# Making the low parts of the weights with an accumulating DMA instead of a subtraction

## The chip, the cores and the metric

The kernel runs on one core of one Trainium2 chip. The metric is the device time of one execution in microseconds, shown as the median of repeated runs. A profile of one execution goes with it: what each engine did and when, what each wait ended on, and what the DMA queues moved.

The engines are named as the profile names them. PE is the matrix engine, with PEld for its weight loads; DVE the vector engine; ACT the scalar engine; POOL the general engine, which can also issue DMAs; SP the engine that here issues all DMAs of the kernel before. Each takes its own instructions strictly in the order in which they were laid down: one that waits holds up all behind it on that engine, while the others go on.

## The reference, cut to what matters

One layer of a decoder over 512 prompt tokens and 32 sample tokens (eight batches of four), all in float32: half a feed-forward block, a mixing layer (half of its heads a recurrent RWKV-7 group, half differential attention), and half a feed-forward block again, with a norm before and after each.

```python
def swiglu(x, w_in, w_out):
    gate, up = jnp.split(x @ w_in, 2, axis=-1)
    return (jax.nn.silu(gate) * up) @ w_out

def layer(x, l, shift0, wkv0, attend, P):
    g = P['norm_gains'][l]
    h = x + 0.5 * rms_norm(swiglu(rms_norm(x, g[0], NORM_EPS), P['ff1_in'][l], P['ff1_out'][l]), g[1], NORM_EPS)
    m, k, v, wkv, shift = mixer(rms_norm(h, g[2], NORM_EPS), l, shift0, wkv0, attend, P)
    h = h + rms_norm(m, g[3], NORM_EPS)
    h = h + 0.5 * rms_norm(swiglu(rms_norm(h, g[4], NORM_EPS), P['ff2_in'][l], P['ff2_out'][l]), g[5], NORM_EPS)
    return h, k, v, wkv, shift
```

Six weight matrices carry the work: `ff1_in`, `ff2_in` (1024 x 5632), `ff1_out`, `ff2_out` (2816 x 1024), `w_in` (1024 x 3328, the projections ahead of the mixer) and `w_out` (1024 x 1024, behind it).

## The kernel before, in words

The 544 tokens are two halves of 272; activations lie with features on the partitions. A weight tile is one block of 128 output features for all its input features, 128 x 1024 float32 (512 KB), or 128 x 768 for the last group of the second feed-forward matrix.

**Two parts for each number.** The matrix engine takes float32r, a shorter form. So every weight and every activation is split in a high part (the value rounded to float32r) and a low part (the value less its high part, rounded too), and a product is the sum of three: high x high, high x low, low x high. `dot` computes one tile's product for one half of the tokens in 24 matmuls: for each of eight 128-row pieces high x high (L130) and high x low (L131), and behind these 16 the eight with the weights' low part (L134). `mm3` (L121 to L123) does the same three piece by piece. So the low part of a weight is wanted only for the last third of a `dot`.

**Making the parts.** `weights` loads a tile into `wraw` (three buffers) by a DMA on SP, lets ACT copy it to `whi` (L114, which rounds), and lets POOL subtract `whi` from `wraw` into `wlo` (L116). `whi` and `wlo` have four buffers each (`wx`, a pool of four more, takes the second half of the tiles in the last group of each feed-forward block). A buffer comes free when the last matmul that reads it is done. For `w_out` the subtraction alternates between DVE and POOL. The first two tiles of the kernel are not made by `weights`, but by hand (L413 to L425).

**The stages.** A feed-forward block (`ff`) goes through 22 blocks of hidden features in three groups. For each hidden block it takes two weight tiles (gate and up), four `dot`s; DVE scales the results (L386, L387), ACT applies Silu (L357), DVE multiplies (L358), ACT and DVE split the hidden rows (L141, L143). After each group, `products` multiplies by the second matrix: eight tiles, two `dot`s each. Between the blocks come the 26 tiles of `w_in` (`proj`, two `dot`s each), mixed with the preparation of the recurrence on DVE (among it the 31 dependent steps of a triangular inverse, L691 and L693), then the recurrence and the attention, which have no weights, and at last `output`: the eight tiles of `w_out` for half 0, and, loaded anew, for half 1, one `dot` for each tile. Its results leave PSUM by ACT (L1224). While half 1 goes through, `close_half` finishes half 0: norm (L276), residual (L277, on POOL for some blocks and on DVE for the others), and the split of the next block's input (L246, L248). `opening` is the first products of a block, with four weight tiles.

**What sets the order.** A scheduler lays down each engine's order from its own estimate of when things are ready; the waits follow from who writes and reads each buffer. So another cost or wait in `weights` also moves instructions elsewhere.

Of the kernel before, what the change touches and what calls it, by code (L numbers as in the profile page):

```python
# [51 lines left out]
def build(ctx, tc, A):  # L52
# [38 lines left out]
    # matmuls ahead of the first data, so that the tensor engine's clock is up when it comes  # L91
# [15 lines left out]
    # ---------------------------------------------------------------- helpers  # L107
    def weights(src, n, wx=None, eng=G, raw=None):
        if raw is None:
            raw = wp.tile([128, n], FT, name="wraw", bufs=3, padded_shape=[128, 1024])  # L110
            nc.sync.dma_start(raw, src)
        slot = dict(bufs=4, padded_shape=[128, n if wx else 1024])
        hi = (wx or wp).tile([128, n], FR, name="whi", **slot)
        S.activation(hi, raw, AF.Copy)  # L114
        lo = (wx or wp).tile([128, n], FR, name="wlo", **slot)
        eng.tensor_tensor(lo, raw, hi.bitcast(FT), op=OP.subtract)  # L116
        return hi, lo

    def mm3(ps, w, x, first, last):
        """ps (+)= w.T @ x, each the exact sum of two float32r parts"""  # L120
# [4 lines left out]
    def dot(ps, w, xs, k0=0, ins=None):  # L125
        """ps = the sum over k of w[k].T @ xs[k], the parts of the weights that come last at the end"""
# [37 lines left out]
    def sums(pt, src, cols):  # L164
        """sums over the partitions that each of cols marks, of a half's tokens, which go on the partitions"""
# [4 lines left out]
    def sums4(ps, bank):  # L170
        """a half's sums, 32 rows (two times 16 alike) for each of four tiles, turned round: [token, tile, block, sum]"""
# [7 lines left out]
    def inv_sqrt(pt, n, scale=1.0, eps=None, least=None, y=None):  # L179
        """(scale * pt + eps) ** -0.5, or of at least `least`: a guess from the exponent, a step of  # L180
        the third order (two thirds of its result), a Newton step"""
# [23 lines left out]
    def spread(y, e, bank=bank):  # L205
        """tokens back to the free axis: each of a token's e values on its share of the partitions, in PSUM"""
# [30 lines left out]
    class Pre:  # L237
        """a block's input, gains applied; the rows' scale is left to whoever takes the product out"""
# [23 lines left out]
    def close_half(h, s, y, sq, gcol, pre=None, xp=None, spill=None, out=None):  # L262
        """the sub-layer's norm and residual, then the next one's input; in steps that other work goes between"""
# [44 lines left out]
    def opening(ws, xs, take):  # L308
        """the first products with a new input: half 1's side by side, as its rows get ready; taken out unscaled"""
# [14 lines left out]
    def products(wsrc, x, y, finish, per=1, wx=None, apart=False):  # L324
        """y[m] for all m and both halves, of weights that hold `per` m each; apart: half 1 after all of half 0"""
# [81 lines left out]
    # ---------------------------------------------------------------- first half-step  # L407
# [46 lines left out]
    # ---------------------------------------------------------------- token mixing  # L454
# [11 lines left out]
    # what lives from the projections to the output product  # L466
# [25 lines left out]
    def projected(i):  # L492
        """block i of the projected RWKV columns, behind the token before: what proj takes, what shifted reads"""
# [28 lines left out]
    def shifted(pr, dst, dsts):  # L522
        """mixed with the token before"""
# [55 lines left out]
    # negated biases over distances  # L579
# [10 lines left out]
    # a row for each partition, so that reading one place earlier on each gives a Toeplitz matrix  # L590
# [5 lines left out]
    for b in range(4):  # L596
# [14 lines left out]
        # decays: products over the chunk, of all tokens up to one and including it  # L611
# [6 lines left out]
        # removal keys, of unit length  # L618
# [11 lines left out]
        # keys and their share  # L630
# [45 lines left out]
    # unit triangular inverses: 32x32 blocks on one partition each, then one merge  # L676
# [25 lines left out]
    def merged():  # L702
        """the inverses' lower left blocks, in steps between the projections"""
# [27 lines left out]
    # queries, and in their place what they attend to  # L731
# [3 lines left out]
    # ---------------------------------------------------------------- RWKV, prompt: chunk after chunk  # L735
# [5 lines left out]
    def ahead(c, bank):  # L741
        """what a chunk needs from its own tokens alone"""
# [22 lines left out]
        # right-hand sides: keys against values  # L765
# [9 lines left out]
    def chunk(c, state, ar, g, kbt, vs, rhs):  # L775
        # the state's part of the right-hand sides
# [14 lines left out]
        # next state  # L791
# [7 lines left out]
        # outputs  # L799
# [11 lines left out]
    # ---------------------------------------------------------------- attention projections  # L811
# [13 lines left out]
    def between(spot):  # L825
        """a step of the inverses' merging behind the products so far"""
        if spot in ((1, 0), (1, 1), (1, 2), (2, 0)):
            with tc.issue_after(latest[0]):
                next(merging, None)
# [41 lines left out]
    # ---------------------------------------------------------------- attention, prompt  # L871
    # lambda
# [11 lines left out]
    # negated biases: one Toeplitz tile for each head  # L884
# [5 lines left out]
    # a head's two queries, each with zeros for the other's rows  # L890
# [40 lines left out]
    # ---------------------------------------------------------------- RWKV, samples: one small chunk  # L931
    sm = att.enter_context(tc.tile_pool(name="smp", bufs=1, side="right", reuse_waits="tile"))

    def sample_steps():
# [14 lines left out]
        # state against keys and queries, value-major: [v, (which, batch, t)]  # L949
# [90 lines left out]
    # ---------------------------------------------------------------- attention, samples  # L1040
    sa = att.enter_context(tc.tile_pool(name="sat", bufs=1, side="right", reuse_waits="tile"))

    def past_steps():
# [12 lines left out]
        # biases of the rows (batch, head, map, t): buckets of all t stacked on the partitions  # L1056
# [23 lines left out]
        def pages(src, n, j0, i):  # L1080
            """two pages of one batch, in a slot of the weights"""
# [315 lines left out]
```

## Time and profile before

| | |
|---|---|
| median of three runs | 1316.78 us (1316.12 to 1322.76) |
| profiled execution, first to last instruction | 1314.4 us |
| PE busy | 1256.5 us, 96% |
| DVE busy | 696.4 us, 53% |
| POOL busy | 503.1 us, 38%; 399.9 of it in L116 |
| ACT busy | 461.2 us, 35%; 182.6 of it in L114 |
| DMA | 142.06 MB, queue q1 34.4% of 16 engines' span |

A row of instruction groups reads: line, engine, operation, output<-inputs, shapes, count | busy us, mean ns of one | idle time of the engine just before, and what ended it. A row of waits reads: who waited, for whom: us in total, times, longest. Time that an engine spends waiting counts only where PE, which has by far the most work, stands still for it.

### The profile page before, as it was taken

The page shows a single profiled execution, that of the slowest core. Times are in us where ns is not written, and L with a number is a line of the kernel's source. Part 1 is how long each engine was busy: PE and PEld are TensorE (multiplying, and loading weights), DVE is VectorE, ACT ScalarE, POOL GpSimd, SP SyncE. Part 2 cuts the span into 40 slices and gives each one's busy share as a digit, 9 for nine tenths or more (in the row PEclk, how much of TensorE's full clock was granted, in tenths as well). Part 3 has the DMA queues.
Part 4 walks back from the last instruction along what each step waited for, and adds up shares of the span by engine and source line. Part 5 has one row for each costly group of instructions (what it writes and reads, how often), then busy time and mean ns, then how long its engine had stood idle before and what let it go on. Part 6 is the DMA issues. An engine that isn't in the chain of part 4 may idle for free.

```text
span 1314.4 us, 25021 instructions
## 1 busy us (share of the span) xinstructions
PE 1256.5 (96%) x10354; PEld 1184.2 (90%) x10354; DVE 696.4 (53%) x1356; ACT 461.2 (35%) x878; POOL 503.1 (38%) x330
## 2 busy tenths in 40 slices
PE   8999999999998989989999999998899999999996
PEld 7999999999998888978887755888899999999995
DVE  7742034412448898879425367788842044412446
ACT  6433232312334444411114446555332233312331
POOL 2534433443346496633000022343534343433342
PEclk8999999999999999899899899999999999999998
DMA  5333223322232423353116357541323322322221
GB/s 198 99 95 97 81 81 97 95 83 81 85 109 87 150 87 124 135 180 110 59 50 190 129 177 262 182 131 47 113 81 97 94 79 86 97 85 79 82 61 68
DMA packets 54455, 142.06 MB, mean 108 GB/s; under 512 B 6050, under 2 KB 17058, under 8 KB 53191
## 3 DMA queue, kind: packets, MB, share of 16 engines
q1 hardware_dynamic: 54342, 140.48, 34.4%
q8 instruction: 81, 1.33, 0.4%
q14 instruction: 32, 0.25, 0.1%
HBM read 125.05 MB, written 16.72 MB: 108 GB/s over the span
## 4 chain that ended last, share of the span: by engine, by line
PE 45%; DVE 9%; ACT 1%; DMA 1%; issue 1%; SPq 0%; DVEq 0%; POOL 0%; ACTq 0%
PE mm L134 7%; PE mm L131 7%; PE mm L130 7%; PE pb L134 3%; PE pb L131 3%; PE pb L130 3%; DVE sqa L228 1%; PE pb L905 1%; DVE tmp L691 1%; PE pb L807 1%; PE pb L806 1%; PE pb L755 1%; DVE X L693 1%; PE pb L927 1%; PE mm L1099 1%
## 5 line engine op out<-in xcount | busy, mean ns | idle before, releaser
L116 POOL TENSOR_TENSOR wlo<-wraw,whi 128x1024 fp32r<-128x1024 f32 (+1 forms) x168 | 399.9, 2384 | 540.7 <-ACT whi L114 488.3
L130 PE MATMUL mm<-xh,whi 128*128 128x272 f32 x1160 | 303.1, 292 | 9.1 <-DVE q_f L820 3.5
L131 PE MATMUL mm<-xl,whi 128*128 128x272 f32 x1160 | 303.5, 293 | 4.7 <-DVE xl L248 4.7
L114 ACT ACTIVATE whi<-wraw 128x1024 fp32r<-128x1024 f32 (+1 forms) x176 | 182.6, 1039 | 253.8 <-PE mm L131 152.0
L130 PEld LDWEIGHTS mm<-xh,whi 128*128 128x128 f32 x1160 | 221.6, 191 | 11.3 <-DVE q_f L820 4.1
L131 PEld LDWEIGHTS mm<-xl,whi 128*128 128x128 f32 x1160 | 221.7, 191 | 6.6 <-DVE xl L248 6.3
L134 PE MATMUL mm<-xh,wlo 128*128 128x272 f32 x1160 | 179.4, 298 | 0.0
L134 PEld LDWEIGHTS mm<-xh,wlo 128*128 128x128 f32 x1160 | 162.8, 197 | 0.3
L130 PE MATMUL pb<-xh,whi 128*128 128x272 f32 x568 | 150.5, 295 | 1.6 <-ACT ga L371 0.9
L131 PE MATMUL pb<-xl,whi 128*128 128x272 f32 x568 | 149.2, 294 | 0.0
L358 DVE TENSOR_TENSOR up<-up,ga 128x272 f32<-128x272 f32 x88 | 111.7, 1271 | 8.2
L130 PEld LDWEIGHTS pb<-xh,whi 128*128 128x128 f32 x568 | 110.3, 194 | 2.8 <-ACT ga L371 1.1
L131 PEld LDWEIGHTS pb<-xl,whi 128*128 128x128 f32 x568 | 109.9, 194 | 0.3 <-issue 0.2
L387 DVE TENSOR_TENSOR up<-mm,rpre 128x272 f32<-128x272 f32 x54 | 23.8, 442 | 114.9 <-PE mm L134 114.8
L134 PE MATMUL pb<-xh,wlo 128*128 128x272 f32 x568 | 83.2, 288 | 0.0
L134 PEld LDWEIGHTS pb<-xh,wlo 128*128 128x128 f32 x568 | 75.6, 188 | 0.0
L357 ACT ACTIVATE ga<-ga 128x272 f32<-128x272 f32 x88 | 38.0, 432 | 71.5 <-DVE ga L386 63.4
L386 DVE TENSOR_TENSOR ga<-mm,rpre 128x272 f32<-128x272 f32 x53 | 23.2, 438 | 73.7 <-PE mm L134 73.7
L130 PE MATMUL mm<-hd0h,whi 128*128 128x272 f32 x242 | 62.0, 289 | 0.0
L131 PE MATMUL mm<-hd0l,whi 128*128 128x272 f32 x242 | 61.9, 288 | 0.0
L130 PE MATMUL mm<-hd1h,whi 128*128 128x272 f32 x220 | 56.4, 289 | 0.0
L131 PE MATMUL mm<-hd1l,whi 128*128 128x272 f32 x220 | 56.3, 288 | 0.0
(406 smaller groups left out, 2277.5 us busy)
## 6 DMA issues: line engine op xcount, KB each, us to landing
wraw<-in_ff_in_dram SPq DMA_DIRECT2D x87, 512.0 KB, 3.6
wraw<-in_ff_out_dram SPq DMA_DIRECT2D x32, 512.0 KB, 3.6
wraw<-in_w_in_dram SPq DMA_DIRECT2D x26, 512.0 KB, 3.9
pg<-in_cache_k_dram SPq DMA_DIRECT2D x32, 256.0 KB, 3.7
pg<-in_cache_v_dram SPq DMA_DIRECT2D x32, 256.0 KB, 5.1
wraw<-in_w_out_dram SPq DMA_DIRECT2D x16, 512.0 KB, 4.1
wraw<-in_ff_out_dram SPq DMA_DIRECT2D x16, 384.0 KB, 3.2
cat_d<-cat SPq DMA_DIRECT2D x4, 1280.0 KB, 5.0
```

The lines of the kernel that those rows point to most:

```text
L114: S.activation(hi, raw, AF.Copy)
L116: eng.tensor_tensor(lo, raw, hi.bitcast(FT), op=OP.subtract)
L130: T.matmul(ps, hi, xs[k][0], start=k == 0, stop=False)
L131: T.matmul(ps, hi, xs[k][1], start=False, stop=False)
L134: latest[0] = T.matmul(ps, wcols(w, k0 + k)[1], xs[k][0], start=False, stop=k == n - 1).ins
L228: eng.tensor_tensor(self.acc, self.acc, sq, op=OP.add)
L357: S.activation(g, g, AF.Silu)
L358: V.tensor_tensor(u, u, g, op=OP.mult)
L386: V.tensor_tensor(g, pg, pre.rs[s], op=OP.mult)
L387: V.tensor_tensor(u, pu, pre.rs[s], op=OP.mult)
L691: V.tensor_tensor(tv, lb[:, j + 1:, j:j + 1].to_broadcast([128, n, m]), X[:, j:j + 1, :m].to_broadcast([128, n, m]), op=OP.mult)
L693: V.tensor_tensor(X[:, j + 1:, :m], X[:, j + 1:, :m], tv, op=OP.subtract)
```

## The change

The low part is no longer computed by an engine. ACT writes the raw weights a second time, times -1 and rounded, into `wlo`: that is minus the high part. Then a DMA issued from POOL reads the raw tile again from DRAM and adds it onto `wlo` in place. Both are the same value as before: raw less high. The options for another engine and for a raw tile that is there already go with it, so `w_out` is treated like the rest. The two tiles made by hand at the start stay as they were. (The new file also drops comments and docstrings; in it the load is L110, the two passes of ACT are L113 and L115, and the DMA is L116.)

```diff
-    def weights(src, n, wx=None, eng=G, raw=None):
-        if raw is None:
-            raw = wp.tile([128, n], FT, name="wraw", bufs=3, padded_shape=[128, 1024])
-            nc.sync.dma_start(raw, src)
+    def weights(src, n, wx=None):
+        raw = wp.tile([128, n], FT, name="wraw", bufs=3, padded_shape=[128, 1024])
+        nc.sync.dma_start(raw, src)
         slot = dict(bufs=4, padded_shape=[128, n if wx else 1024])
         hi = (wx or wp).tile([128, n], FR, name="whi", **slot)
         S.activation(hi, raw, AF.Copy)
         lo = (wx or wp).tile([128, n], FR, name="wlo", **slot)
-        eng.tensor_tensor(lo, raw, hi.bitcast(FT), op=OP.subtract)
+        S.activation(lo, raw, AF.Copy, scale=-1.0)
+        G.dma_start(lo, src, accum_op=OP.add)
         return hi, lo
...
-            w = weights(A["w_out"][m], 1024, eng=(V, G)[m % 2])
+            w = weights(A["w_out"][m], 1024)
```

The order on ACT in the middle of the first feed-forward block, before and with the change (`ga` and `up` are the two hidden tiles, `hd0h` and `hd1h` the high parts of the hidden rows of the two halves):

```order
L357 ACTIVATE ga<-ga 128x272
L141 ACTIVATE hd0h<-up 128x272
L114 ACTIVATE whi<-wraw 128x1024
L357 ACTIVATE ga<-ga 128x272
L114 ACTIVATE whi<-wraw 128x1024
L141 ACTIVATE hd1h<-up 128x272
```

```order
L357 ACTIVATE ga<-ga 128x272
L141 ACTIVATE hd0h<-up 128x272
L113 ACTIVATE whi<-wraw 128x1024
L115 ACTIVATE wlo<-wraw 128x1024
L357 ACTIVATE ga<-ga 128x272
L113 ACTIVATE whi<-wraw 128x1024
L115 ACTIVATE wlo<-wraw 128x1024
L141 ACTIVATE hd1h<-up 128x272
```

Each tile's second pass stands right behind its first; the Silu and the split of the hidden rows stand behind both.

ACT again, in `output` for half 0 (`my` are its results, `sq` their squares), before and with the change:

```order
L1224 ACTIVATE my_1_9641<-pb 128x272
L227 ACTIVATE sq<-my_1_9641 128x272
L114 ACTIVATE whi<-wraw 128x1024
L1224 ACTIVATE my_2_9642<-mm 128x272
L227 ACTIVATE sq<-my_2_9642 128x272
```

```order
L113 ACTIVATE whi<-wraw 128x1024
L1224 ACTIVATE my_1_9733<-mm 128x272
L115 ACTIVATE wlo<-wraw 128x1024
L227 ACTIVATE sq<-my_1_9733 128x272
L113 ACTIVATE whi<-wraw 128x1024
```

Here the second pass stands behind the copy of a product out of PSUM.

POOL from the first tiles of `w_out` to the first of `ff2_in` (`yr` is the recurrence's output, `h` the residual), before and with the change:

```order
L116 TENSOR_TENSOR wlo<-wraw,whi 128x1024
L1192 TENSOR_TENSOR yr<-yr,gor 128x272 x2
L116 TENSOR_TENSOR wlo<-wraw,whi 128x1024 x3
L277 TENSOR_TENSOR h_9928<-h_9928,pn 128x272
L116 TENSOR_TENSOR wlo<-wraw,whi 128x1024
L277 TENSOR_TENSOR h_9928<-h_9928,pn 128x272 x2
L116 TENSOR_TENSOR wlo<-wraw,whi 128x1024
L277 TENSOR_TENSOR h_9928<-h_9928,pn 128x272
```

```order
L1192 TENSOR_TENSOR yr<-yr,gor 128x272 x6
L116 DMA wlo<-in_w_out_dram 128x1024 x12
L277 TENSOR_TENSOR h_10028<-h_10028,pn 128x272 x3
L116 DMA wlo<-in_ff_in_dram 128x1024
L277 TENSOR_TENSOR h_10028<-h_10028,pn 128x272
L116 DMA wlo<-in_ff_in_dram 128x1024 x3
```

The residual of half 0 (L277), which had stood between the subtractions, stands behind the last DMA for `w_out`.

## The prediction

> **What bounds the kernel now.** The page first: busy shares. Then the table by stretches, cut where the stages change (per row: PE's busy time and matmuls, then PEld, DVE, ACT, POOL, the granted clock, the DMA engines' share, GB/s).
>
> ```profile
> PE 1256.5 (96%) x10354; PEld 1184.2 (90%) x10354; DVE 696.4 (53%) x1356; ACT 461.2 (35%) x878; POOL 503.1 (38%) x330
> ...
> 40.00:400.00 360.00, 359.37 (x2869) 359.16 (x2867) 135.23 (x200) 111.21 (x177) 150.63 (x65) 1.00 0.32 91
> 400.00:640.00 240.00, 214.66 (x1810) 203.89 (x1811) 202.20 (x391) 84.66 (x146) 129.58 (x141) 0.93 0.38 124
> 640.00:800.00 160.00, 160.00 (x1679) 116.97 (x1679) 72.54 (x231) 61.93 (x183) 11.59 (x16) 0.97 0.45 141
> 800.00:960.00 160.00, 146.91 (x1065) 130.87 (x1064) 127.15 (x252) 82.83 (x170) 66.12 (x37) 0.98 0.41 130
> 960.00:1280.00 320.00, 320.00 (x2555) 320.00 (x2555) 107.34 (x168) 94.40 (x147) 129.04 (x56) 1.00 0.29 85
> ```
>
> In the two feed-forward blocks PE never stops, so nothing that POOL or DVE saves there can be seen. One matmul comes every 320/2555 = 0.125 us: a `dot` of 24 is 3.0 us, a tile with two `dot`s 6.0 us. PE stands still for 25.3 us between 400 and 640 (projections, recurrence's preparation) and for 13.1 us between 800 and 960 (output product, opening of the second block); there DVE is busy for 84% and 79%. The waits of PE in these two stretches, longest first:
>
> ```profile
> PE pb L214 <- DVE rx L209: 5.7, 3, 2.0
> PE pb L214 <- DVE ry L202: 4.0, 2, 2.2
> PE mm L130 <- DVE q_f L820: 3.5, 3, 1.7
> PE mm L131 <- DVE xl L248: 3.4, 2, 2.4
> PE pb L709 <- DVE lb L697: 2.8, 1, 2.8
> ...
> PE pb L255 <- DVE sqa L228: 2.6, 1, 2.6
> PE pb L168 <- DVE sqa L228: 2.3, 1, 2.3
> PE mm L130 <- DVE ga L386: 1.9, 1, 1.9
> ```
>
> These rows are 26.2 us, all on DVE. No row of PE waits for POOL, and none for the low part of a weight. So the subtractions of POOL, though 400 us long, are hidden; what they cost, they cost through DVE:
>
> ```profile
> L116 POOL TENSOR_TENSOR wlo<-wraw,whi 128x1024 fp32r<-128x1024 f32 (+1 forms) x168 | 399.9, 2384 | 540.7 <-ACT whi L114 488.3
> L358 DVE TENSOR_TENSOR up<-up,ga 128x272 f32<-128x272 f32 x88 | 111.7, 1271 | 8.2
> ...
> 28.60 0.44 DVE L358 TENSOR_TENSOR up<-up,ga 128x272 f32<-128x272 f32 x1
> ...
> 589.83 2.39 DVE L693 TENSOR_TENSOR X<-X,tmp 128x135 f32<-128x135 f32 x1
> 592.25 0.32 DVE L691 TENSOR_TENSOR tmp<-lb,X 128x156 f32<-128x156 f32 x1
> ...
> 589.67 2.40 POOL L116 TENSOR_TENSOR wlo<-wraw,whi 128x1024 fp32r<-128x1024 f32 x1 [3.77 <-PE mm L134]
> ```
>
> The multiplication L358 takes 0.44 us at 28.60, where POOL is idle, and 1.27 us in the mean. At 589.83 a step of the inverse that is smaller than its neighbour takes 2.39 us instead of 0.3: it started 0.16 us after a subtraction on POOL and ended with it. A DVE operation with two inputs in SBUF that meets a subtraction waits until that is over.
>
> **The subtractions go.** 168 on POOL and 8 on DVE (in `output`). On POOL this is off the path: worth nothing by itself. Through DVE, bounds: nothing, if PE's waits have other causes, and all 26.2 us of the rows above. The longest waits are 1.7 to 2.8 us each, about one blocked operation (2.1 us in the pair at 589.83); 26 and 21 subtractions fall in the two stretches, and without them DVE still has 202 - 26 x 2.1 = 147 us of work in the 240 of the first. I take two thirds: **-18 us**.
>
> **ACT's second pass.** 176 more passes of 1.04 us:
>
> ```profile
> L114 ACT ACTIVATE whi<-wraw 128x1024 fp32r<-128x1024 f32 (+1 forms) x176 | 182.6, 1039 | 253.8 <-PE mm L131 152.0
> ...
> 942.94 1.01 PE mm L134 x8
> ```
>
> 183 us on an engine that is busy for 461 of 1314. In 960 to 1280 it is 2555/48 = 53 tiles, 55 us on top of 94 in 320: hidden under PE; without that cover it would be 1 us per tile. The added wait: L115 needs the buffer of `wlo`, free after the last L134, while L113 needs that of `whi`, free after the last L131. The eight L134 take 1.01 us, L113 itself 1.04, so L115 finds it free. Behind both in the feed-forward blocks stand the Silu and the split of the hidden rows, then DVE's L143, then the products, which come a group later: nothing. In `output` the copies out of PSUM (L1224) stand between the passes, and three PSUM buffers of 3 us each cover a delay of 1 us. **0**, up to +2 where PE has just lost its lead.
>
> **The DMA's load.** A second read of 176 tiles, now with an addition. No row shows such a DMA. The plain one:
>
> ```profile
> q1 hardware_dynamic: 54342, 140.48, 34.4%
> ...
> wraw<-in_ff_in_dram SPq DMA_DIRECT2D x87, 512.0 KB, 3.6
> ...
> wraw<-in_w_out_dram SPq DMA_DIRECT2D x16, 512.0 KB, 4.1
> ...
> h_d<-h SPq DMA_DIRECT2D x2, 1088.0 KB, 10.8
> h<-h_d SPq DMA_DIRECT2D x2, 1088.0 KB, 5.2
> ```
>
> Of the 16 engines, 0.344 x 1314.4 us went for 140.48 MB, so 1.69 us for 0.524 MB. The addition reads the tile from DRAM, reads `wlo` and writes it: at least one pass (1.69), at most three one after the other (5.07). I take two, 3.4 us, since a plain load's read and write are one pass already and one read comes on top. Then a tile takes 1.69 + 3.4 = 5.1 of PE's 6.0 us: hidden, at 85% of the DMA engines. At three it is 6.8 and the DMA engines become the bound (below).
>
> The Trainium skill has a price (Collectives: The Full Stack, "The bandwidth ceiling"): an adding DMA is slower not for the addition but for its two source reads on one ring, 62.28 against 32.35 GB/s, 1.93 times. By it, as an estimate, the tile would take 1.69 + 3.26 = 4.95 us, and the sum stays. No run here shows it yet.
>
> **The DMA's delay.** The low part was there 2.39 us after the high one; now it takes L115, an issue on POOL and a landing. Bounds for the landing: 3.6 us (a plain load) and 10.8 us (the slowest row, twice the bytes). I take 7, twice the plain load. What it may take follows from four buffers. In a feed-forward block a buffer of the first tile of a pair is free after the third of four `dot`s (9.0 us), and its next low part is wanted 16 matmuls into the next pair but one (24 + 2.0): 17 us, less 1 for L115. In `output`, with one `dot` for each tile, it is free after 3.0 and wanted at 12 + 2.0: 11 us, less L115 and the copy ahead of it (0.4): 9.5. So 7 us is hidden in both; at 10.8 `output` loses 1.3 us in each round of four, 5 us in all.
>
> The cover is thin where a block opens, since all four tiles are wanted at once. At the start of the program:
>
> ```profile
> 17.18 1.05 ACT L114 ACTIVATE whi<-wraw 128x1024 fp32r<-128x1024 f32 x1
> ...
> 23.16 1.17 PE L134 MATMUL pb<-xh,wlo 128*128 128x272 f32 x8
> ```
>
> Ready now at 17.18 + 2.1 + 7 = 26.3, wanted at 23.16: 3 us late, which products of the other half can fill in part. Three such openings: **+3** (0 to 9). In `output` the DMA engines, at 0.41 of 160 us before, get 21 tiles' additions of 3.4 us on top (0.86), and loads that DVE waits for (the recurrence's rows) share them; POOL's residual of half 0 now comes behind twelve DMAs, each waiting for ACT. **+5** (0 to 20).
>
> ```profile
> SPq L111 <- POOL wlo L116: 789.8, 149, 26.1
> ```
>
> SP's loads wait for POOL to be done with `wraw`; now ACT releases it 1.3 us earlier. The loads are a buffer ahead anyway: nothing.
>
> **Sum**: -18 + 0 + 3 + 5 = -10 us on a profiled span of 1314.4, so 1304.4. The median of the runs is 2.4 us above that span; against it the forecast is 1307 us.
>
> **Rivals.** *The saving stays on DVE.* PE's waits end on DVE, but the chain in front of them is long, and what DVE wins is lost at the openings and behind the second pass: 1316. For it: in 400 to 640 transfers stand in the chain of waits too:
>
> ```profile
> 572.68 7.28 DMA bon_d<-bon
> 580.46 3.86 DMA ar<-cat_d
> ```
>
> Against it: the inverse, a pure DVE chain, with single steps of 2.1 us too much.
>
> *The low parts come late.* One mechanism, in `output` and the three openings: landing over 9.5 us, because the additions queue with the loads at 85% load. At 14 us, four rounds of 4.5 us in `output` and 7 us more at each opening are 18 + 21 = 39, against -10: about 1345. For it: the store of 10.8 us, and DMA shares of 0.38 to 0.45 ahead of the change in the middle stages. Against it: loads that land in 3.6 us at today's load.
>
> *The addition takes three passes.* From 4.3 us per tile on (6.0 - 1.69) the feed-forward blocks hang on the DMA engines; at 5.07 each of their 136 tiles takes 0.78 us longer: +106, with -10 about 1412. For it: no row shows an addition. Against it: nothing but the count of reads.
>
> *The change does not free DVE*, since POOL's writing of descriptors blocks it too: the -18 goes, 1324. By the Trainium skill (SBUF — State Buffer, "Who interferes with whom") a DVE operation with two SBUF inputs meets only a GpSimd instruction that reads SBUF, not one that only writes: this rival would then be out. The trace shows the reading half (589.83, 2.39 us) alone.
>
> **How the numbers follow.** Forecast 0.47, saving stays on DVE 0.18, low parts late 0.20, three passes 0.10, DVE not freed 0.05. The likeliest has its own range of 1290 to 1311: from all 26.2 us with no loss, to 6 us left of them. The range to hold 8 of 10 goes down to 1290 and up to 1365, past the late low parts and short of three passes. About 0.5% (6.6 us) is what a measurement of this kernel tells from no change. Faster by more: 0.45, the forecast without its upper rim. Slower by more: 0.20 + 0.10 and a part of the two cases near zero, 0.34. Within: 0.21.
>
> **What would show it.** Right: L358's mean falls from 1.27 to under 0.6 us; in 400 to 640 and 800 to 960 PE's busy time rises by 12 us or more together, and its waits on DVE shrink; the feed-forward stretches stay at 0.125 us per matmul; POOL's busy time is near 100 us, ACT's near 644. The step on load: the DMA share in 960 to 1280 near 0.29 x 3 = 0.87; over 0.95 with PE waiting is three passes. The step on delay: additions that land in 7 us; a PE wait named for L134 and `wlo` means late low parts. The forecast falls if PE's waits on DVE stay as they are, or new ones on DMAs come to more than they lose.

## The result, and the profile after

The changed kernel takes 1338.61 us (median of four runs, 1333.09 to 1340.21) against 1318.97 us before: a ratio of 1.0139, 95% interval 1.011 to 1.0169. It is 1.4% slower; the forecast was 0.7% faster. The profiled execution spans 1338.5 us.

From the page of the changed kernel, and for L358 from its groups of DVE: the busy shares, groups of instructions, DMA queues (packets, MB, share of 16 engines' span) and DMA issues (count, KB each, median us from issue to landing).

```profile
PE 1275.5 (95%) x10354; PEld 1194.5 (89%) x10354; DVE 527.3 (39%) x1348; ACT 618.0 (46%) x1054; POOL 249.9 (19%) x338
...
L115 ACT ACTIVATE wlo<-wraw 128x1024 fp32r<-128x1024 f32 (+1 forms) x176 | 181.5, 1033 | 5.8 <-PE mm L134 5.0
L116 POOL DMA_DIRECT2D wlo<-in_ff_in_dram x86 | 74.6, 871 | 416.9 <-ACT wlo L115 402.6
...
L358 DVE TENSOR_TENSOR up<-up,ga 128x272 f32<-128x272 f32 x88 | 38.8, 442 | 8.5 <-ACT ga L357 0.5
...
q0 software_dynamic: 25344, 90.19, 36.4%
...
wraw<-in_ff_in_dram SPq DMA_DIRECT2D x87, 512.0 KB, 5.2
wlo<-in_ff_in_dram POOLq DMA_DIRECT2D x86, 512.0 KB, 7.9
...
wlo<-in_w_in_dram POOLq DMA_DIRECT2D x26, 512.0 KB, 8.9
...
wraw<-in_w_out_dram SPq DMA_DIRECT2D x16, 512.0 KB, 8.6
```

DVE is freed as forecast: L358 takes 442 ns, not 1271, and DVE is busy 169 us less. ACT's second passes are 181.5 us; as neighbouring rows overlap a little, ACT is busy 156.8 us more. The additions cost 0.364 x 1338.5 us of the 16 engines for 90.19 MB, 2.83 us for a tile of 0.524 MB, and land 7.6 to 8.9 us after their issue. The plain loads land later than before, too: 5.2 us in place of 3.6 for `ff_in`, 8.6 in place of 4.1 for `w_out`.

The table by stretches, columns as in the prediction:

```profile
0.00:40.00 40.00, 31.74 (x179) 29.40 (x180) 24.91 (x57) 26.28 (x54) 5.33 (x8) 0.83 0.75 216
40.00:400.00 360.00, 356.12 (x2834) 355.68 (x2834) 86.22 (x196) 162.96 (x233) 54.53 (x63) 1.00 0.80 179
400.00:640.00 240.00, 229.63 (x2068) 218.30 (x2068) 167.88 (x407) 115.17 (x182) 84.93 (x141) 0.96 0.68 184
640.00:800.00 160.00, 158.81 (x1493) 113.58 (x1490) 63.79 (x210) 56.26 (x170) 11.38 (x16) 0.87 0.42 138
800.00:960.00 160.00, 138.03 (x919) 117.42 (x918) 81.53 (x237) 100.90 (x190) 35.60 (x42) 0.93 0.75 199
960.00:1280.00 320.00, 320.00 (x2555) 320.00 (x2554) 74.91 (x171) 142.24 (x201) 45.86 (x53) 1.00 0.78 175
```

In 400 to 640 PE stands still for 10.4 us in place of 25.3, and does 258 matmuls more. In 640 to 800, where there are no weights but the last of `w_in` and the first of `w_out`, it does 186 fewer, at a granted clock of 0.87 in place of 0.97. In 800 to 960 it stands still for 22.0 us in place of 13.1. The middle of the second feed-forward block (960 to 1280) goes on at 2555 matmuls. PE's waits:

```profile
PE pb L134 <- DMA wlo<-in_ff_in_dram: 6.3, 3, 2.4
PE mm L1205 <- ACT fsq L1204: 5.4, 2, 3.6
PE pb L134 <- DMA wlo<-in_ff_out_dram: 5.1, 2, 3.1
PE mm L134 <- DMA wlo<-in_w_in_dram: 4.8, 2, 3.3
...
PE mm L134 <- DMA wlo<-in_w_out_dram: 3.5, 5, 2.0
PE mm L134 <- DMA wlo<-in_ff_in_dram: 3.1, 2, 1.8
PE mm L134 <- DMA wlo<-in_ff_out_dram: 3.1, 2, 1.9
...
PE pb L134 <- DMA wlo<-in_w_out_dram: 2.7, 3, 1.5
```

The seven rows on `wlo` are late low parts, 28.6 us together; no such row existed before, when the rows on DVE made up most of PE's waits. But they mostly take the place of those: over the whole profile PE stands still for 63.0 us (span less busy time) in place of 57.9. The span, and the mean granted clock (the share of its full speed that PE was given), before and after:

```profile
core 0: 1314.4 us, clock 0.973
```

```profile
core 0: 1338.5 us, clock 0.959
```

Of the 24.1 us that the profile is longer, 19.0 are PE's busy time for the same 10354 matmuls, at the lower clock; busy time times clock is the same in both (1256.5 x 0.973 = 1222.6, 1275.5 x 0.959 = 1223.2). The prediction's sum is made of waits and has no term for the clock.

**By stages.** Fixed stretches shift against each other, so the runs below are compared by seven stages, each from one product of PE's to another: S1 the first feed-forward block, to its last product with hidden rows (416.5 us before); S2 projections and the recurrence's preparation, to the first L709 (210.0); S3 recurrence, to the first L1066 (75.4); S4 attention, to the first product with rows of `output` (121.1); S5 `output`, to the last of these (62.3); S6 opening and first hidden group of the second feed-forward block (112.7); S7 the rest of that block, to its last product (301.6). Differences to the kernel before, in us, each of one profiled execution. An execution lies anywhere in its kernel's scatter, which goes with the granted clock (the kernel before takes 1315 to 1318 us at 0.974 and 1326 to 1330 at 0.963), so 2 or 3 us in a stage are not a finding, and more where the profiled execution is far from its kernel's median: e8's is 6 us above it, those of e7, e9, e10, e12 and e13 are 3, 7, 2, 3 and 11 us below.

| | S1 | S2 | S3 | S4 | S5 | S6 | S7 |
|---|---|---|---|---|---|---|---|
| the change | +8.0 | -17.2 | +2.3 | +15.7 | +8.3 | +2.0 | +4.9 |

The gain is there, in S2. Of the 41.2 us lost elsewhere 18.0 are in S3 and S4, where few weights are made or used: the last projections and the first tiles of `w_out`.

### The profile page after: what moved, and what is told of

It is laid out like the page before. It is cut to its first block, busy times and chain, and to the rows that moved or that the text cites. A ratio compares the mean times of both kernels' runs of the same rounds, so it can differ in the third digit from the quotient of the medians.

```text
span 1338.5 us, 25334 instructions
## 1 busy us (share of the span) xinstructions
PE 1275.5 (95%) x10354; PEld 1194.5 (89%) x10354; DVE 527.3 (39%) x1348; ACT 618.0 (46%) x1054; POOL 249.9 (19%) x338
## 3 DMA queue, kind: packets, MB, share of 16 engines
q0 software_dynamic: 25344, 90.19, 36.4%
## 4 chain that ended last, share of the span: by engine, by line
PE 82%; DMA 6%; issue 5%; DVE 4%; ACT 1%; POOL 1%; SPq 0%; POOLq 0%; DVEq 0%; ACTq 0%
PE mm L134 15%; PE mm L131 14%; PE mm L130 14%; PE pb L130 7%; PE pb L131 7%; PE pb L134 7%; DMA wlo<-in_ff_in_dram 2%; PE pb L755 1%; DMA wlo<-in_ff_out_dram 1%; PE pb L807 1%; PE pb L905 1%; PE pb L806 1%; POOL wlo L116 1%; DMA bonr<-bon_d 1%; PE mm L1099 1%
## 5 line engine op out<-in xcount | busy, mean ns | idle before, releaser
L113 ACT ACTIVATE whi<-wraw 128x1024 fp32r<-128x1024 f32 (+1 forms) x176 | 182.9, 1040 | 230.4 <-PE mm L131 71.9
L115 ACT ACTIVATE wlo<-wraw 128x1024 fp32r<-128x1024 f32 (+1 forms) x176 | 181.5, 1033 | 5.8 <-PE mm L134 5.0
L116 POOL DMA_DIRECT2D wlo<-in_ff_in_dram x86 | 74.6, 871 | 416.9 <-ACT wlo L115 402.6
L130 PE MATMUL pb<-xh,whi 128*128 128x272 f32 x568 | 147.8, 291 | 1.6 <-ACT ga L371 0.9
L116 POOL DMA_DIRECT2D wlo<-in_ff_out_dram x48 | 41.6, 872 | 214.0 <-ACT wlo L115 209.2
L141 ACT ACTIVATE hd0h<-up 128x272 fp32r<-128x272 f32 x44 | 19.0, 431 | 116.3 <-DVE up L358 116.3
```

The costliest lines, as they stand in the source:

```text
L115: S.activation(lo, raw, AF.Copy, scale=-1.0)
L116: G.dma_start(lo, src, accum_op=OP.add)
L130: T.matmul(ps, hi, xs[k][0], start=k == 0, stop=False)
L141: S.activation(hi, src, AF.Copy)
```

## The experiments

In kernels with added lines the line numbers are 3 (e1 to e3) or 7 (e5 to e12) higher; in `weights` itself, for e5 to e12, L117 and L122 are ACT's two passes. Diffs are abridged. Each median is set against the kernel before on the same chip in the same set (1320.26, 1319.95, 1322.01 and 1320.40 us for e1 to e4, e5 to e8, e9 to e12, e13 and e14).

### First set: one place or one part at a time, the scheduler free

The option for another engine comes back into `weights`, and the call sites choose:

```diff
-    def weights(src, n, wx=None):
+    def weights(src, n, wx=None, eng=None):
...
-        S.activation(lo, raw, AF.Copy, scale=-1.0)
-        G.dma_start(lo, src, accum_op=OP.add)
+        if eng is None:
+            S.activation(lo, raw, AF.Copy, scale=-1.0)
+            G.dma_start(lo, src, accum_op=OP.add)
+        else:
+            eng.tensor_tensor(lo, raw, hi.bitcast(FT), op=OP.subtract)
```

**e1, the middle of the feed-forward blocks.** `eng=G` at the openings, `w_in` and each block's last group, `eng=(V, G)[m % 2]` at `w_out`.

> The accumulating DMA only in the middle of the feed-forward blocks (112 of 176 tiles); the openings, w_in, w_out and each block's last group keep the subtraction. Theory A (low parts that land too late, where there is little lead): none is late here, and no saving on DVE counts in these stretches; time as before within 4 us (1315 to 1323 against 1319), no PE wait named for wlo. Theory B (the DMA load as such, through slower loads or through PE's clock, wherever it is): 112/176 of the 20 us lost, +13, about 1332, with the mean granted clock below that of before by about 0.01.

Measured 1342.1 us, ratio 1.0151 (1.0116 to 1.0185). Theory A falls: nothing was changed between the end of the first block and the opening of the second, and yet S3 and S4 are 7.4 and 8.5 us longer. Theory B fails too: in 960 to 1280 the DMA share is 0.77 and PE does its 2555 matmuls as before. The lower clock that it expects is there (0.962 over the span), but the fall is in 640 to 800 us (0.87 in place of 0.97), where nothing was added.

**e2, `w_in` behind its opening.** `eng` given everywhere else.

> The accumulating DMA only for the 22 tiles of w_in behind its opening. Theory A: DVE is freed in 400 to 640 us as in the whole change (PE idle there 25 down to 10 us), few late low parts, nothing changed elsewhere: 10 to 15 us faster, 1304 to 1309. Theory B: 22/176 of 20 us, +2.5, less the gain. A third view (what DVE wins in this stretch is given back by PE's clock or by the stages behind it): within 4 us of before.

Measured 1316.0 us, 0.9947 (0.9912 to 0.9982): S2 is 17.3 us shorter, S3 and S4 2.9 and 8.5 us longer. The third view holds (4.3 us under the kernel before, where it allows 4): most of the gain is given back by stages that the edit does not touch.

**e3, `w_out`.** `eng=G` everywhere else.

> The accumulating DMA only for the 16 tiles of w_out (8 of their subtractions had been on DVE). Theory A: low parts come late with one product per tile; PE waits named for wlo<-in_w_out of 5 to 8 us, against 3 to 5 us that DVE wins: 0 to 8 us slower, 1319 to 1327. Theory B: +2 us, no such waits.

Measured 1332.3 us, 1.0087 (1.0061 to 1.0113), above theory A's bound. S5 +10.9 with 7.8 us of waits for `wlo`, which theory A does expect; again S4 +6.9.

**e4, the second pass without the DMA.**

```diff
-        G.dma_start(lo, src, accum_op=OP.add)
+        G.tensor_tensor(lo, raw, lo.bitcast(FT), op=OP.add)
```

> ACT's second pass everywhere, but POOL adds the raw tile onto the negated high part in place of the DMA: the second pass alone, with the old load on POOL and DVE's port. The prediction's step (the second pass is hidden, 0 to +2 us): 1319 to 1322. A rival (ACT's passes delay the copies out of PSUM in the output product and the openings, so that a good part of the loss is ACT's): 1325 to 1335, with PE waits on ACT.

Measured 1347.0 us, 1.0177 (1.0128 to 1.0225): at least about as slow as the whole change (the intervals overlap), and not by any DMA. S3 +9.9, S4 +15.3.

All four lose in S3 and S4, whatever they change. What they share is that the scheduler, with other costs before it, laid down another order. That makes a theory C: the order itself costs time.

### Second set: the order held

The program is built twice. The first build gives each engine's order; in the second, every instruction is queued behind its predecessor in that order (a rule of issue alone, no wait for an end). PE's order in e5 is then that of the kernel before, row by row but for two neighbours. A second pass goes right behind its first, a DMA where its subtraction stood; for the eight `w_out` tiles that DVE had subtracted, it goes where the scheduler puts it. The kernel before with its own order held was not run, but stages that an edit leaves alone keep their length (S7 in e8, e9, e10 and e12: 0.0).

```diff
+    order = the engines' orders of a first build
+    for row in order: for a, b in zip(row, row[1:]): tc.add_manual_dep(b, a, NoSync)
```

**e5, the change in the old order; e6, the subtractions in the new order; e7, e4 in the old order; e8, e2 in the old order.**

> The whole change, but each engine's order of instructions held as in the kernel before (each second pass right behind its first, each DMA where its subtraction stood on POOL). Theory A (late low parts and the load of the DMA cost the time): as slow as the change or slower, 1335 to 1350, attention stage (first page scores to first output product) no longer than the 121 us of before but the openings and output longer. Theory C (the scheduler's new order of the mixing layer costs most of it, which fits that the stages without weights lost 8 to 16 us in all runs so far): attention back to 121 us, projections still 17 us shorter, 1305 to 1320.

> The subtractions of the kernel before, no DMA and no second pass, but each engine's order held as in the changed kernel. Theory A: as the kernel before, 1315 to 1325. Theory C: slower by what attention and the stages around it lost, 1330 to 1345, with the attention stage at 130 us or more without any change in how the low parts are made.

> ACT's second pass with POOL adding, in the order of the kernel before: the price of ACT's passes alone. The prediction's step and theory C: 0 to +4 us (1319 to 1323), since 1347 in its own order came from the order. Rival: ACT's passes themselves cost the 27 us, 1335 to 1350.

> The accumulating DMA only for w_in behind its opening, in the order of the kernel before. Theory C: the 17 us that the projections won without the 11 us that attention and its output lost: 1302 to 1308, faster than both kernels. Rival (attention follows from PE's state and the earlier work, not from the order): 1314 to 1318 as in its own order.

| | us | ratio (95%) | S1 | S2 | S3 | S4 | S5 | S6 | S7 |
|---|---|---|---|---|---|---|---|---|---|
| e5 change, old order | 1335.3 | 1.0098 (1.0064 to 1.0132) | +17.0 | -13.6 | -1.7 | +8.4 | +10.3 | -3.5 | +6.6 |
| e6 before, new order | 1340.8 | 1.0154 (1.0122 to 1.0186) | +1.5 | +1.3 | +7.3 | +11.1 | -1.6 | +1.4 | +3.7 |
| e7 ACT's pass, POOL adds, old order | 1341.2 | 1.0169 (1.0137 to 1.0201) | +4.4 | -0.2 | -0.5 | +2.7 | +7.4 | +7.3 | +1.2 |
| e8 `w_in`, old order | 1301.2 | 0.985 (0.9819 to 0.9881) | +0.7 | -10.5 | -3.3 | +1.5 | 0.0 | +3.0 | 0.0 |

**e6** is theory C as it stands: the kernel before, with its own subtractions, becomes 20.8 us slower by the order of the changed kernel alone, and 18.4 us of its profile's loss are S3 and S4. As in the changed kernel most of it is not waiting: PE stands still for 64.7 us (57.9 before) and is busy for 17.8 us more, at a mean clock of 0.959. **e8** is the other side: the same edit as e2, 15 us faster in the old order, and faster than both kernels.

**e5** shows that theory C is only half: the change loses 15.3 us in the old order too, in theory A's range and not in C's. S3 is back at its length, but S1, S5 and S7 lose 34 us, and S4 8.4. Its longest waits:

```profile
PE pb L141 <- DMA wlo<-in_ff_in_dram: 8.7, 2, 5.3
PE pb L929 <- DVE sc L922: 6.2, 1, 6.2
PE pb L141 <- DMA wlo<-in_ff_out_dram: 6.1, 2, 3.8
PE mm L141 <- DMA wlo<-in_ff_in_dram: 5.7, 3, 4.5
```

Single waits for a low part are up to 5.3 us here, where those of the changed kernel are 3.3 at most. The scheduler's new order may have moved work in front of the late low parts (S1 +8.0 in place of +17.0) and paid for it in the mixing layer; that is argued from the stages, and no run shows it.

**e7** goes against theory C and the prediction at once: ACT's second pass, with no DMA and in the old order, costs 21.3 us. Its places are S5 and S6. The stretch there, of e7, and behind it the chain of waits (start, us, what):

```profile
878.00:905.00 27.00, 23.25 (x172) 22.01 (x171) 20.66 (x36) 20.92 (x37) 18.24 (x10) 0.96 0.39 117
```

```profile
878.56 1.03 ACT whi L117
...
883.48 0.95 ACT whi L117
884.43 0.94 ACT wlo L122
885.73 2.48 DVE sqa L235
...
904.96 1.04 ACT wlo L122
906.35 2.47 DVE sqa L235
```

ACT is busy 20.92 of 27 us, the squares of the norm stand behind its passes, DVE's sum of squares (L235, still 2.5 us long, since POOL still computes the low parts) behind these. PE waits for the copies out of PSUM as well, a row that the kernel before does not have:

```profile
PE mm L137 <- ACT my L1231: 1.8, 2, 1.0
```

Part of the 21 us may be POOL's, though, which here makes all sixteen low parts of `w_out`.

### Third set: what is left, in the old order

**e9, all subtractions on POOL.**

```diff
-            w = weights(A["w_out"][m], 1024, eng=(V, G)[m % 2])
+            w = weights(A["w_out"][m], 1024, eng=G)
```

> The kernel before in its own order, but the eight subtractions of w_out that were on DVE are on POOL, as the change takes them off DVE; no second pass, no DMA. It splits the 21 us of ACT's second pass with POOL adding. If the passes of ACT cost it: 1318 to 1325 here. Rival (POOL, which has to make all sixteen low parts of w_out, is what is late there, not ACT): 1328 to 1336, with the output stage 4 us longer or more.

Measured 1330.5 us, 1.0054 (1.0031 to 1.0076); S5 +3.7, S4 +1.7, S6 +1.9. That is in the rival's range: eight subtractions more on POOL cost 8.5 us. What e7 has beyond it is ACT's second pass, with POOL's work behind it: 21.3 - 8.5 = 13 us (15 by the two ratios). So e7's loss is both. In the same place as above e9's ACT is busy 15.87 of 27 us, so 5 us of passes had been added in these 27:

```profile
869.00:896.00 27.00, 23.96 (x188) 23.31 (x186) 24.22 (x38) 15.87 (x32) 18.54 (x11) 0.99 0.43 134
```

**e10, `w_in` without its first tile.** The DMA for 21 tiles: of `w_in`, all but the opening's four and the next one. `weights` is told the kind of its tile; `n` counts its calls:

```diff
+        if (kind == "w_in" and n >= 71):  # e11: or kind in ("hidden", "out"); e12: kind == "w_out"
+            S.activation(lo, raw, AF.Copy, scale=-1.0)
+            G.dma_start(lo, src, accum_op=OP.add)
+        else:
+            eng.tensor_tensor(lo, raw, hi.bitcast(FT), op=OP.subtract)
```

> The accumulating DMA for 21 tiles of w_in, without the first one behind the opening, in the order of the kernel before. If the one wait of 4.8 us for that tile's low part, and the clock that falls behind it, are a loss of their own: 4 to 8 us under the 1301 of the kernel with 22 tiles, 1293 to 1298. Rival (the next tile is late in its place): 1299 to 1303.

Measured 1298.9 us, 0.9831 (0.9794 to 0.9869): the fastest kernel here, 23 us under the one before. S2 is 19.7 us shorter, S3 4.7; S6 is 4.6 longer. PE's wait for low parts in e8, and in e10:

```profile
PE mm L141 <- DMA wlo<-in_w_in_dram: 4.8, 1, 4.8
```

```profile
PE mm L141 <- DMA wlo<-in_w_in_dram: 2.4, 2, 1.8
```

The wait halves rather than goes, since the next tiles' low parts are late in their turn: both expectations are part right. Against its own before e10 gains 4 us more than e8, which the runs' scatter (1296 to 1308 in e8) hardly tells from nothing. In the profiles S2 is 9.2 us shorter, but e8's is the slowest of its six runs and e10's the fastest of its own.

**e11, subtractions at the late places alone.** The DMA for e10's tiles and, in both feed-forward blocks, behind the opening up to the last group's products.

> The accumulating DMA for 133 of 176 tiles, in the order of the kernel before: the middle of both feed-forward blocks and w_in behind its first tile; subtractions where the low part is wanted soon (openings, first tile of w_in, w_out, each block's last group). Theory A+C (in the middle of the feed-forward blocks neither ACT's pass, nor the DMA's load, nor its landing costs anything; the order cost the 22 us there): within 4 us of the kernel with w_in alone, 1293 to 1302. Theory B (load and passes cost wherever they are): 112/176 of the 15 us that the change cost in the old order, +10 on it, 1304 to 1312.

Measured 1306.1 us, 0.9861 (0.9824 to 0.9898): a time in theory B's range, but not lost where theory B has it. S3 to S5 are as in e10 to the tenth, and S7 as before: second passes and additions at a DMA share of 0.70 cost nothing in a running block. The loss against e10 is in S1 (+9.6, e10 +1.6) and S2 (2.8 us). PE's waits name two places in the feed-forward blocks:

```profile
PE mm L141 <- DMA wlo<-in_ff_in_dram: 4.5, 1, 4.5
PE pb L141 <- DMA wlo<-in_ff_in_dram: 4.3, 1, 4.3
```

Both are the first pair behind an opening (at 51.5 and 918.2 us). An opening uses its four tiles side by side and frees all four buffers at its very end, so the tiles behind it have no lead, just as the opening itself has none. In the second block this costs nothing more, since there e10's PE waits 3.4 us for DVE anyway.

**e12, `w_out`, in the old order.**

> The accumulating DMA for the 16 tiles of w_out alone, in the order of the kernel before (the DMAs of the eight tiles that DVE had subtracted stand where the scheduler puts them). The prediction's step: +5 less what DVE wins there, 1319 to 1325, output stage 62 to 68 us. Theory A: the output stage as long as with the whole change, +8 to +12: 1327 to 1334, with PE waiting for wlo<-in_w_out.

Measured 1337.4 us, 1.0127 (1.0087 to 1.0168): S5 +9.9, S4 +6.4. That is above both ranges. PE's waits for `wlo<-in_w_out` are only 3.1 us, so theory A has the direction and not the mechanism. S4's end, in e12: POOL's part of it (start, us, and in brackets the wait before), the wait of ACT, and landings of the recurrence's rows in 800 to 860 us:

```profile
815.94 0.75 POOL L1199 TENSOR_TENSOR yr<-yr,gor 128x272 f32<-128x272 f32 x1 [1.57 <-DVE z L920]
825.23 0.76 POOL L1199 TENSOR_TENSOR yr<-yr,gor 128x272 f32<-128x272 f32 x1 [8.54 <-DMA gor<-bon_d]
```

```profile
826.02 0.43 ACT L1200 ACTIVATE orp<-yr 128x272 fp32r<-128x272 f32 x1 [7.16 <-POOL yr L1199]
```

```profile
wlo<-in_w_out_dram POOLq DMA_DIRECT2D x8, 512.0 KB, 8.7
...
bonr<-bon_d SPq DMA_DIRECT2D x7, 136.0 KB, 9.9
gor<-bon_d SPq DMA_DIRECT2D x7, 136.0 KB, 5.0
```

and the same rows of the kernel before:

```profile
bonr<-bon_d SPq DMA_DIRECT2D x7, 136.0 KB, 3.2
gor<-bon_d SPq DMA_DIRECT2D x7, 136.0 KB, 3.0
```

The recurrence's rows are loaded while the first tiles of `w_out` are, and the additions are in the same DMA engines. The rows land in 9.9 us (`bonr`) and 5.0 (`gor`) in place of 3.2 and 3.0; POOL waits 8.5 us for one of them, ACT's split of the recurrence's output (L1200) waits 7.2 us for POOL, and behind it on ACT stands what attention still needs. That is S4. In S5 it is a raw tile of `w_out` that lands late, and ACT waits 5.6 us for it. Both are among the longest pieces of e12's chain of waits:

```profile
811.68 13.41 DMA gor<-bon_d
...
848.61 13.29 DMA wraw<-in_w_out_dram
```

By this trace the additions cost less by their own landing than by that of the plain loads beside them. No run takes the late loads alone away, and the 15.4 us hold the sixteen second passes on ACT too.

### Fourth set: how the order costs

**e13, only recurrence and attention in the old order.** The change as it is, but between the recurrence's start and `output` the instructions other than second passes and the DMAs of low parts keep the kernel before's relative order.

```diff
+    order = {e: [k for k in row if k in inside] for e, row in order.items()}
```

> The whole change in the scheduler's own order, but the instructions of the recurrence and the attention (which use no weights of their own; the second passes, DMAs and products of w_out are left free) held in the relative order of the kernel before. If the new order of this part costs the 18 us that the changed kernel lost from the inverse to the first output product (and the kernel before in the new order as well): about 1321, with 75 and 121 to 128 us for these two stages in place of 77.7 and 136.8. Rival (the loss there comes from the whole order, or from the second pass and the DMAs that reach into it): 1333 to 1340.

Measured 1328.9 us, 1.0066 (1.0041 to 1.0092), between the two: 9.7 us under the changed kernel. Its profiled execution, 1315.7 us, is the fastest of its seven, so its stages (S3 -5.0, S4 +8.2) show the place and not the size. The order of this part is about half of the change's loss. The part held is wider than the expectation says: the twelve projections of attention, tiles of `w_in`, are in it.

What the order changes there, by PE's groups in the 44 us behind the last projections, in the kernel before (690 to 734 us) and in e6 (696 to 740):

```profile
L905 PE MATMUL pb<-k_f,qpad 128*128 128x256 f32 (+1 forms) x20 | 5.6, 386 | 0.0
...
L1099 PE MATMUL mm<-pg,qz 128*32 128x256 f32 x32 | 3.4, 494 | 0.0
```

```profile
L912 PE MATMUL pb<-k_f,qpad 128*128 128x256 f32 x12 | 4.1, 452 | 0.0
```

The recurrence's chunks are nearly the same in both; but before, 20 matmuls of scores and 32 with cached keys stand between them, and in the new order 12 and none (L912 is L905). The attention's products come later, and the chunks' small products of 64 x 64 follow each other alone.

**e14, large products between the small ones.** In e6, with products that nobody reads added:

```diff
+    def fill(ps, c):
+        if c:
+            T.matmul(ps, ones, cst[:, :512], start=True, stop=True)
...
         ps = bank()
+        fill(ps, c)
```

> The kernel before in the new order (1341 us), with 14 products of 128x128 by 128x512 that nobody reads put between the recurrence's small products (64 x 64), two in each chunk but the first; at full clock one takes about 0.53 us, 7.5 us in all. If PE's clock falls there because the recurrence's small products follow each other without large ones: the granted clock of 700 to 760 us rises from 0.74 to 0.9 or more, and the time falls or stays, 1328 to 1342. Rival (the clock there follows something else): clock as before, 1346 to 1352.

Measured 1348.7 us, 1.0223 (1.0195 to 1.0252). The stretch 690 to 750 of the kernel before, then 700 to 760 of e6 and of e14:

```profile
690.00:750.00 60.00, 60.00 (x672) 44.14 (x670) 26.15 (x96) 26.40 (x83) 3.01 (x8) 0.94 0.57 175
```

```profile
700.00:760.00 60.00, 60.00 (x537) 43.26 (x535) 19.68 (x71) 20.83 (x66) 0.00 (x0) 0.74 0.35 101
```

```profile
700.00:760.00 60.00, 60.00 (x581) 42.14 (x580) 23.05 (x84) 20.42 (x64) 3.00 (x8) 0.94 0.35 106
```

The added products in e14:

```profile
L787 PE MATMUL pb<-cst,ones 128*128 128x512 f32 x28 | 15.7, 641 | 0.0
```

The clock rises from 0.74 to 0.94, as the theory has it, and the time lies in the rival's range. But the expectation priced the 14 products at half of what they take: each is two matmuls in the trace, and together they keep PE busy for 15.7 us, not 7.5. All of them are in S3 and S4, and these are together only 2.9 us longer than in e6; the whole kernel is 7.9 us longer (6 of them in S2, which the edit leaves alone and which ran at a lower clock, 0.91 in place of 0.93 in 400 to 640 us). So the better clock gave back about 8 us by the medians and 13 by the two stages, of the 18 that these lose in e6. The low clock goes with the thin order and is about half of its price or more, as far as one profile of each kernel tells. That the rest is attention started later, with less left to overlap, is argued from the counts above and not shown.

## Why the prediction was wrong

**Right.** *The subtractions go*, -18: S2 alone is 17.2 us shorter, and the DMA for 21 tiles of `w_in` gains 23 us (e10), near the upper bound of 26.2. L358 at 442 ns, POOL's issues notwithstanding, puts out the rival in which DVE is not freed. *The DMA's load*, two passes of 1.69: 2.83 us, 1.68 passes; 0.78 of the DMA engines in 960 to 1280 (0.87 forecast), hidden. The ratio in the Trainium skill ("Collectives: The Full Stack", "The bandwidth ceiling": 1.93 for two reads on one ring) is 15% above the 1.68 measured here. *The landing* of 7 us: 7.6 to 8.9. *Feed-forward*: 0.125 us per matmul, unchanged (e11, S7). Of the other signs that were named, three did not come: PE's busy time in 400 to 640 and 800 to 960 rose by 6.1 us together (15.0 more and 8.9 less) and not by 12; POOL is busy for 249.9 us and not 100, since its 176 DMA issues count 0.87 us each; ACT for 618.0 and not 644. In the rival with three passes a tile is 0.76 us longer by its own figures (1.69 + 5.07 - 6.0), not 0.78, which changes nothing.

**ACT's second pass, 0 to +2: wrong, it is 13 to 15 us** (e7 less e9, with POOL adding in place of the DMA). The step took PSUM's three buffers as cover in `output`. PE does wait for those copies in e7 (1.8 us). And what stands behind the passes there is not only the copies, but the norm's squares and the splits of the next block's input, on which PE waits next; and ACT, at 35% over the whole span before, is at 20.9 of 27 us in that place with the second pass. The share of the span hid the stage.

**Three openings, +3 (0 to 9): too small.** The tiles behind an opening are as bare as the opening, which the step did not count. Together these are the waits of e11 (4.5 and 4.3) and of e8 (4.8), besides those of the openings proper.

**`output`, +5 (0 to 20): 15.4 us** (e12, ACT's second passes on these tiles included), in the range and for a reason that the step named ("loads that DVE waits for share them"), but put at a third of its size: the recurrence's rows at 9.9 us in place of 3.2, through POOL and ACT to PE, and a late raw tile. The slack of 9.5 us that was worked out for the low part itself held nearly: 3.1 us of waits in e12, 6.2 in the changed kernel. The other reason named, POOL's residual behind twelve DMAs, shows in the changed kernel (the last of them goes out at 892.09 us, POOL's first residual starts at 892.65), but no run gives its price.

**The step that was missing: the order.** The pieces of the order were shown, and every term was then worked out as if each stage kept its own. The new order costs the kernel before 20.8 us by itself (e6), its part from the recurrence through attention about 10 us of the change's loss (e13). Most of that (17.8 of the 24.6 us that e6's profile is longer) is no wait at all, but PE at a lower granted clock, for which the sum had no place although its own table showed 0.93 to 1.00 by stretch. These do not add up with the terms above: in the old order the change still costs 15.3 us (e5), in the new one 19.6. How the two meet (work moved in front of late low parts, at the mixing layer's expense) is argued and stays open.

**The rivals.** "The low parts come late" (1345) is nearest to the 1338.6, with late low parts worth 28.6 us of waits, but at landings of 8 to 9 us, not 14, 8.2 of the 28.6 at `ff_out`, which it did not name, and about as much time saved in waits on DVE. That its number is near is luck: the mechanism behind most of it is the order. "The saving stays on DVE" had the openings and the second pass as places of loss, rightly, but not their size. "Three passes" and "DVE not freed" are out by the rows above.

## What to carry to other kernels

Price a change by stages, and give the instruction order its own term: where a scheduler lays it down from estimates, hold the old order once (and try the old code in the new order) before a difference is put down to the edit. Take work off an engine only where that engine is waited for, and where the slower replacement has lead: 21 of 176 tiles, in the old order, gave 23 us, and all of them together cost 15 there. Look at PE's busy time and clock, and not at its waits alone: the same matmuls can take longer. A buffer group that is freed all at once leaves the tiles behind it without lead.

## What the runs showed of the hardware

- A DMA that adds into SBUF takes 2.83 us of the 16 DMA engines for 512 KB, against 1.69 for a plain load, and occupies POOL for 0.87 us per issue; a DVE operation with two SBUF inputs is not held up by it (442 ns).
- Plain loads beside it land later: `ff_in` after 5.2 us in place of 3.6, `w_out` after 8.6 in place of 4.1, rows of 136 KB (in e12) after 9.9 in place of 3.2.
- In all fifteen kernels without added products PE's busy time times its mean granted clock is 1220 to 1226 us, with busy times from 1248.7 us (clock 0.979, e10) to 1283.9 (0.952, e4).
- PE's granted clock was 0.74 in the mean over 60 us in which the profile shows PE busy all the time, mostly with small products (64 x 64), and 0.94 over the same 60 us with 8 of the 14 added products of 128x128 by 128x512 among them (16 rows of L787 in e14). The Trainium skill ("TensorE: Matmul & The Clock Gate", "Part 1: The HAM clock gate (the "warmup" mystery)") has the clock fall after an idle window of about 3.4 us; here it falls where the profile shows none. That small products do not count as full work is what e14 suggests.
